# A convolution with residual on one core: first load on one ring, 4 MB residual loads and stores, fewer semaphores

## The chip, the cores and the metric

The kernel runs on one core of one Trainium2 chip. The time is the device time in microseconds. A profile is one execution, and its span, from the first to the last instruction of the program, is some 1.9 us shorter than the time (121.2 us against 123.0 for the profiled execution before). All instants below are microseconds from the span's start. PE runs the matmuls, ACT and DVE cast and add, GpSimd (POOL) makes constants and clears semaphores, and SP issues transfers. A "ring" is the queue of transfers of one issuing engine; in the profiles q1 is that of SP and q10 that of ACT.

## The reference

A 3x3 convolution with padding 1, batch 16, 64 channels in and out, 64x64 pixels, all float32, plus a residual of the output's shape:

```python
x_pad = np.pad(x, ((0, 0), (0, 0), (pad, pad), (pad, pad)), mode='constant')
...
output[b, co] += weight[co, ci, kh, kw] * x_pad[b, ci, kh:kh+h, kw:kw+w]
...
return (output + residual).astype(np.float32)
```

x, the residual and the output have 16.8 MB each; the weights have 0.15 MB. So 50.48 MB cross between HBM and the core, in either kernel.

## The kernel before

The images go in pairs: two images of 64 channels fill the 128 partitions, so one pair of x, of the residual or of the output is 2 MB (128 rows of 16 KB). ACT casts x to bf16 in two halves per image, PE makes six accumulating groups of four matmuls per image in one of two halves of PSUM, and DVE adds PSUM to the residual in place with two instructions per image. SP issues nearly all transfers, in the program's order:

```python
def load_x(p, engine=nc.sync, cols=slice(0, NPIX)):
    return engine.dma_start(out=xr[p % NXR][:, cols], in_=x_bc[128 * p : 128 * p + 128, cols]).then_inc(
        s_x[p % NXR], 16
    )

def load_ro(p):
    nc.sync.dma_start(out=ro[p][:, :], in_=res_bc[128 * p : 128 * p + 128, :]).then_inc(s_r[p], 16)

def store(p):
    return nc.sync.dma_start(out=out_bc[128 * p : 128 * p + 128, :], in_=ro[p][:, :])
# ... cut ...
for p in range(NPAIR):                       # NPAIR = 8, NXR = 3 buffers of x
    if p >= NXR:
        nc.sync.wait_ge(s_half, 2 * (p - NXR) + 3)   # ACT is done with the buffer
    if p == 0:
        to_the_front(load_x(p, cols=slice(0, NPIX // 2)))
        nc.sync.dma_start(out=wraw[:, :], in_=w_rows[:, :]).then_inc(s_w, 16)
    else:
        load_x(p)
    load_ro(p)
for p in range(NEARLY):                      # NEARLY = 6
    nc.sync.wait_ge(s_add, 2 * p + 3)
    store(p).then_inc(s_out, 16)
# ... cut: GpSimd's constants ...
to_the_front(load_x(0, nc.scalar, slice(NPIX // 2, NPIX)))   # the second half, on ACT's ring
# ... cut: ACT's casts, DVE's adds, PE's loop ...
for p in range(NEARLY, NPAIR):               # after the critical section
    store(p)
with tc.tile_critical(sync_engine=mybir.EngineType.Pool, no_gpsimd_drain=True):
    nc.gpsimd.wait_ge(s_out, 16 * NEARLY)
```

`to_the_front` moves a load ahead of the program's first barrier, so that it starts at once. After the program's last transfer come two barriers of all engines with a clear of the kernel's semaphores between them, which the language adds.

## Time and profile before

| | before |
|---|---|
| time, median of 3 runs | 123.09 us (122.86 to 123.21) |
| span | 121.2 us |
| PE, DVE, ACT busy | 72%, 63%, 52% |
| bytes between HBM and core, mean over the span | 50.48 MB, 417 GB/s |
| DMAs of the program | 26 (x 9, weights 1, residual 8, output 8) |
| last add ends, last two stores issued | 104.1; 104.4 and 104.8 |
| last two stores landed | 115.4 and 120.2 |

The timeline of the kernel before, from the last adds on, without the sequencers' waits (start, duration, engine and line, operation, count):

```profile
99.52 4.61 DVE L201 TENSOR_TENSOR ro<-ps,ro 64x2048 f32<-64x2048 f32 x2 [0.58 <-PE ps L86]
104.42 0.96 SPq L79 DMA_DIRECT2D out_dram<-ro  x2
```

The reader is to see that no engine works after 104.1, and that issuing the last two stores takes SP less than a microsecond. The remaining 16 us hold no instruction that computes; they are all transfers. The prediction below shows the page's slices and reads them.

### The profile page before, as it was taken

What the parts mean: (1) busy time and instruction counts of PE and PEld (TensorE: products, weight loads), DVE (VectorE), ACT (ScalarE), POOL (GpSimd) and SP (SyncE); (2) the same over time, 40 slices, a digit from 0 to 9 for tenths busy, and PEclk for the clock granted to TensorE, in tenths of its full rate; (3) what the DMA queues carried; (4) which work ended last, traced back from release to release, by engine and by line L of the source; (5) the groups of instructions that cost most, each with busy time, mean ns of one, the idle gap of its engine ahead of it and who ended that gap; (6) DMA issues with size and microseconds to landing.
All of it is one profiled execution on the core that took longest, in us unless ns stands there. A gap on an engine that the chain in (4) does not pass through costs nothing.

```text
span 121.2 us, 736 instructions
## 1 busy us (share of the span) xinstructions
PE 87.7 (72%) x389; PEld 10.7 (9%) x105; DVE 76.0 (63%) x40; ACT 63.1 (52%) x37; POOL 2.4 (2%) x16
## 2 busy tenths in 40 slices
PE   0033499999999999999999999999999980000000
PEld 0021001101010101010101010101010100000000
DVE  0005300889898898989889898898989889300000
ACT  4049969938966984993993994896000000000000
POOL 5200000000000000000000000000000000000000
PEclk9999999999999999999999999999999999755555
DMA  6999999999999999999999999999999999999993
GB/s 168 427 444 433 433 433 433 433 427 433 433 427 427 433 433 427 427 433 427 433 433 433 433 433 422 433 389 433 433 433 433 422 433 433 433 433 433 427 433 151
DMA packets 3744, 50.48 MB, mean 417 GB/s; under 512 B 416, under 2 KB 544, under 8 KB 544
## 3 DMA queue, kind: packets, MB, share of 16 engines
q1 hardware_dynamic: 3600, 49.43, 96.3%
q10 hardware_dynamic: 144, 1.05, 2.0%
HBM read 33.70 MB, written 16.78 MB: 417 GB/s over the span
## 4 chain that ended last, share of the span: by engine, by line
PE 71%; DVEq 2%; DVE 2%; issue 0%
PE ps L86 53%; PE ps L85 17%; DVEq L129 2%; DVE ro L201 2%
## 5 line engine op out<-in xcount | busy, mean ns | idle before, releaser
L201 DVE TENSOR_TENSOR ro<-ps,ro 64x2048 f32<-64x2048 f32 x32 | 73.2, 2289 | 17.7 <-PE ps L86 17.2
L86 PE MATMUL ps<-xp,wl 128*128 128x504 bf16 (+1 forms) x288 | 80.0, 388 | 0.2
L173 ACT CAST xp<-xr 64x2048 bf16<-64x2048 f32 x16 | 30.3, 1896 | 19.3 <-DMA xr<-in_x_dram 17.1
L85 PE MATMUL ps<-xp,wl 128*128 128x504 bf16 (+1 forms) x92 | 35.8, 389 | 3.4 <-PEq L222 3.4
L177 ACT CAST xp<-xr 64x2048 bf16<-64x2048 f32 x16 | 30.4, 1897 | 0.4
L85 PEld LDWEIGHTS ps<-xp,wl 128*128 128x128 bf16 x96 | 9.5, 99 | 79.1 <-issue 79.1
L189 DVE CAST wl<-ps 32x192 bf16<-32x192 f32 x8 | 2.8, 348 | 10.4 <-PE ps L214 10.3
L214 PE MATMUL ps<-ident,wraw 128*32 128x128 f32 x9 | 2.1, 412 | 8.1 <-DMA wraw<-in_weight_dram 8.1
L214 PEld LDWEIGHTS ps<-ident,wraw 128*32 128x32 f32 x9 | 1.2, 137 | 8.6 <-issue 8.1
L173 ACT ACT_TABLE_LOAD x1 | 1.3, 1283 | 1.1 <-SPq L129 1.1
L182 ACT CAST wl<-ps 32x192 bf16<-32x192 f32 x4 | 1.2, 306 | 0.0
L160 POOL MEMSET xp<- 64x64 bf16 x4 | 0.6, 147 | 0.2
L159 POOL MEMSET xp<- 64x64 bf16 x4 | 0.6, 145 | 0.2
L148 POOL TENSOR_SCALAR_AFFINE_SELECT ident<-ident 128x128 f32<-128x128 f32 x1 | 0.3, 295 | 0.2 <-POOL ident L146 0.2
L162 POOL MEMSET wl<- 64x192 bf16 x1 | 0.3, 253 | 0.1
L161 POOL MEMSET wl<- 64x192 bf16 x1 | 0.3, 252 | 0.1
L146 POOL MEMSET ident<- 128x128 f32 x1 | 0.2, 205 | 0.7 <-SPq L129 0.7
L257 POOL MEMSET const-uint8-127<- 128x1 uint8 x1 | 0.1, 113 | 0.0
L257 POOL MEMSET const-bfloat16-1.0<- 128x1 bf16 x1 | 0.1, 112 | 0.0
L257 POOL MEMSET const-float32-1.0<- 128x1 f32 x1 | 0.1, 109 | 0.0
L257 POOL MEMSET const-float32-0.0<- 128x1 f32 x1 | 0.1, 104 | 0.2 <-issue 0.2
## 6 DMA issues: line engine op xcount, KB each, us to landing
ro<-in_residual_dram SPq DMA_DIRECT2D x8, 2048.0 KB, 21.9
out_dram<-ro SPq DMA_DIRECT2D x8, 2048.0 KB, 28.2
xr<-in_x_dram SPq DMA_DIRECT2D x7, 2048.0 KB, 17.5
xr<-in_x_dram SPq DMA_DIRECT2D x1, 1024.0 KB, 7.0
xr<-in_x_dram ACTq DMA_DIRECT2D x1, 1024.0 KB, 7.6
wraw<-in_weight_dram SPq DMA_DIRECT2D x1, 144.0 KB, 6.9
```

Of the source, the lines that this page charges most:

```text
L85: return e.matmul(out=out_, lhsT=lhsT, rhs=rhs, start=start, stop=stop, skip_group_check=True)
L86: return e.add_instruction(mybir.InstMatmult(name=nc.get_next_instruction_name(), engine=PE, ins=[e.lower_ap(rhs), e.lower_ap(lhsT)], outs ...
L129: with tc.tile_critical(no_gpsimd_drain=True):
L159: nc.gpsimd.memset(t[0:64, 0, :], 0.0).then_inc(s_id, 1)
L160: nc.gpsimd.memset(t[64:128, J, :], 0.0).then_inc(s_id, 1)
L173: i = nc.scalar.copy(out=t[64:128, 0:J, :], in_=x4[hp, :, 0, :])
L177: nc.scalar.copy(out=t[0:64, 1 : J + 1, :], in_=x4[hp, :, 1, :]).then_inc(s_pack, 1)
L182: i = nc.scalar.copy(**weight_block(h, *b))
L189: i = nc.vector.tensor_copy(**weight_block(h, *b))
L201: i = nc.vector.tensor_tensor(out=o4[hp, :, par, :], in0=psj[64 * par : 64 * par + 64, :, :], in1=o4[hp, :, par, :], op=ADD)
L214: i = nc.tensor.transpose(out=tp[0:32, t // 3, 128 * (t % 3) : 128 * (t % 3) + 128], in_=wraw3[:, :, t], identity=ident[:, :])
L257: nc = _bacc.Bacc("TRN2", target_bir_lowering=False, num_devices=1)
```

## The change

The intent was to hand the same bytes to the transfers in fewer pieces: a first load of x on one ring, residual loads and early stores of two pairs (4 MB), fewer semaphores, and a clear of the user's semaphores on GpSimd while the last stores still run. The core of the diff:

```diff
-    NEARLY = 6
+    NEARLY = 3
+    RES = (slice(0, 1), slice(1, 2), slice(2, 4), slice(4, 6), slice(6, 8))
-    res_bc = residual.rearrange("b c h w -> (b c) (h w)")
+    res_bc = residual.rearrange("(p b) c h w -> (b c) p (h w)", b=2)
-    ro = [pool.tile([128, NPIX], FP32, name=f"ro{p}") for p in range(NPAIR)]
+    ro = pool.tile([128, NPAIR, NPIX], FP32)
-    s_r = [sem(f"s_r{p}") for p in range(NPAIR)]
+    s_r = [sem(f"s_r{i}") for i in range(2)]
-    s_wt = sem("s_wt")
...
+    def load_ro(i):
+        if i >= 2:
+            nc.sync.wait_ge(s_r[i % 2], 16 * (i // 2))
+        nc.sync.dma_start(out=ro[:, RES[i], :], in_=res_bc[:, RES[i], :]).then_inc(s_r[i % 2], 16)
+    def store(pairs):
+        return nc.sync.dma_start(out=out_bc[:, pairs, :], in_=ro[:, pairs, :])
...
-                to_the_front(load_x(p, cols=slice(0, NPIX // 2)))
+                to_the_front(load_x(p))
...
-            load_ro(p)
-        for p in range(NEARLY):
-            nc.sync.wait_ge(s_add, 2 * p + 3)
-            store(p).then_inc(s_out, 16)
+            if p in (0, 1, 3, 5, 7):
+                load_ro((p + 1) // 2)
+        for k in range(NEARLY):
+            nc.sync.wait_ge(s_add, 4 * k + 5)
+            store(slice(2 * k, 2 * k + 2)).then_inc(s_out, 16)
...
-        to_the_front(load_x(0, nc.scalar, slice(NPIX // 2, NPIX)))
...
         nc.gpsimd.wait_ge(s_out, 16 * NEARLY)
+        tc.free_semaphores([s_w, *s_x, *s_r, s_out, s_id, s_half, s_pack, s_bank, s_conv, s_add])
```

The cuts hold the same change for the output's view, the use of `s_id` in place of `s_wt`, and the indices that follow from them.

More of the change, by code (lines that the diff above doesn't have):

```diff
@@ L37 @@
     NXP = 4
-    NEARLY = 6
-    res_bc = residual.rearrange("b c h w -> (b c) (h w)")
-    out_bc = out.rearrange("b c h w -> (b c) (h w)")
+    NZERO = 4 + 2 * NXP
+    NEARLY = 3
+    RES = (slice(0, 1), slice(1, 2), slice(2, 4), slice(4, 6), slice(6, 8))
+    res_bc = residual.rearrange("(p b) c h w -> (b c) p (h w)", b=2)
+    out_bc = out.rearrange("(p b) c h w -> (b c) p (h w)", b=2)
     x_bc = x.rearrange("b c h w -> (b c) (h w)")
@@ L68, with load_x @@
     s_add = sem("s_add")
-    def load_x(p, engine=nc.sync, cols=slice(0, NPIX)):
-        return engine.dma_start(out=xr[p % NXR][:, cols], in_=x_bc[128 * p : 128 * p + 128, cols]).then_inc(
-            s_x[p % NXR], 16
-        )
-    def load_ro(p):
-        nc.sync.dma_start(out=ro[p][:, :], in_=res_bc[128 * p : 128 * p + 128, :]).then_inc(s_r[p], 16)
-    def store(p):
-        return nc.sync.dma_start(out=out_bc[128 * p : 128 * p + 128, :], in_=ro[p][:, :])
+    def load_x(p):
+        return nc.sync.dma_start(out=xr[p % NXR][:, :], in_=x_bc[128 * p : 128 * p + 128, :]).then_inc(s_x[p % NXR], 16)
+    def load_ro(i):
[4 more added lines that the diff above has]
+        return nc.sync.dma_start(out=out_bc[:, pairs, :], in_=ro[:, pairs, :])
     def matmul(out_, lhsT, rhs, start, stop, ldweights):
@@ L171 @@
             if im == 0:
-                nc.scalar.wait_ge(s_x[p % NXR], 16 * (p // NXR + 1 + (p % NXR == 0)))
+                nc.scalar.wait_ge(s_x[p % NXR], 16 * (p // NXR + 1))
             i = nc.scalar.copy(out=t[64:128, 0:J, :], in_=x4[hp, :, 0, :])
@@ L178 @@
             if n == 0:
-                nc.scalar.wait_ge(s_wt, 1)
+                nc.scalar.wait_ge(s_id, NZERO + 1)
                 for b in blocks[4:]:
@@ L182 @@
                         i = nc.scalar.copy(**weight_block(h, *b))
-                i.then_inc(s_wt, 1)
-        nc.vector.wait_ge(s_wt, 1)
+                i.then_inc(s_id, 1)
+        nc.vector.wait_ge(s_id, NZERO + 1)
         for k, b in enumerate(blocks[:4]):
@@ L191 @@
                     i.then_inc(s_bank, 2)
-        i.then_inc(s_wt, 1)
+        i.then_inc(s_id, 1)
         for n in range(B):
@@ L195 @@
             hp = slice(64 * im, 64 * im + 64)
-            o4 = ro[p].rearrange("q (j two w) -> q j two w", two=2, w=W)
+            o4 = ro[:, p, :].rearrange("q (j two w) -> q j two w", two=2, w=W)
             psj = ps[n % 2].rearrange("q c j w -> q (c j) w")
             if im == 0:
-                nc.vector.wait_ge(s_r[p], 16)
+                i = next(i for i, pairs in enumerate(RES) if p < pairs.stop)
+                nc.vector.wait_ge(s_r[i % 2], 16 * (i // 2 + 1))
             for par in range(2):
@@ L207 @@
                 i.then_inc(s_add if par == 0 or n == B - 1 else s_bank, 1)
-        nc.tensor.wait_ge(s_id, 4 + 2 * NXP)
+        nc.tensor.wait_ge(s_id, NZERO)
         nc.tensor.wait_ge(s_w, 16)
@@ L216 @@
             )
-        i.then_inc(s_wt, 1)
-        nc.tensor.wait_ge(s_wt, 3)
+        i.then_inc(s_id, 1)
+        nc.tensor.wait_ge(s_id, NZERO + 3)
         with nc.Fori(0, B // NXP, 1, engines=[PE]):
@@ L236 @@
                 m.then_inc(s_conv, 1)
-    for p in range(NEARLY, NPAIR):
-        store(p)
+    for p in range(2 * NEARLY, NPAIR):
+        store(slice(p, p + 1))
     with tc.tile_critical(sync_engine=mybir.EngineType.Pool, no_gpsimd_drain=True):
         nc.gpsimd.wait_ge(s_out, 16 * NEARLY)
+        tc.free_semaphores([s_w, *s_x, *s_r, s_out, s_id, s_half, s_pack, s_bank, s_conv, s_add])
 _INS = ['x', 'weight', 'residual']
```

## The prediction

> **What bounds the kernel now.** I read the page's slices first, because the ladder of engines (PE 72%, DVE 63%, ACT 52%) names no engine that is full. The slices and the queue table do:
>
> ```profile
> PE   0033499999999999999999999999999980000000
> DVE  0005300889898898989889898898989889300000
> DMA  6999999999999999999999999999999999999993
> GB/s 168 427 444 433 433 433 433 433 427 433 433 427 427 433 433 427 427 433 427 433 433 433 433 433 422 433 389 433 433 433 433 422 433 433 433 433 433 427 433 151
> ...
> q1 hardware_dynamic: 3600, 49.43, 96.3%
> q10 hardware_dynamic: 144, 1.05, 2.0%
> ```
>
> The reader is to see that DMA stands at 9 in every slice but the first and the last, at about 433 GB/s, while PE is idle in the last seven slices and DVE in the last five. The chain of work on the page says "PE 71%", but it follows instructions only; it stops at the last stores' issue and doesn't see that these stores then queue behind others. The DMA queue's own waits and the stretches show that:
>
> ```profile
> SPq L268 <- DMA out_dram<-ro: 14.8, 2, 10.0
> ```
>
> ```profile
> 1.00:2.00 1.00, 0.00 (x0) 0.00 (x0) 0.00 (x0) 0.92 (x1) 0.59 (x3) 1.00 1.06 197
> 2.00:3.00 1.00, 0.00 (x0) 0.00 (x0) 0.00 (x0) 0.36 (x1) 0.73 (x6) 1.00 0.84 311
> 3.00:4.00 1.00, 0.00 (x0) 0.00 (x0) 0.00 (x0) 0.00 (x0) 0.78 (x5) 1.00 1.00 418
> ...
> 110.00:115.00 5.00, 0.00 (x0) 0.00 (x0) 0.00 (x0) 0.00 (x0) 0.00 (x0) 0.50 0.99 423
> ```
>
> The last add ends at 104.1 us and the last two stores are issued at 104.42 and 104.80, yet they land at 115.4 and 120.2, because earlier stores (2 MB each, 4.85 us from one landing to the next) still stand in front: the sixth lands at 110.5. So compute has about 5 us of slack at the end: a 2 MB store whose data reaches the queue before the sixth store leaves it, near 110, costs nothing.
>
> The account of the 121.2 us is then: first packet at 1.0 us after the span's start; 50.48 MB at the steady 433 GB/s, which is 116.6 us; a ramp (197, 311 and 418 GB/s in the three microseconds from 1.0 on) that loses (236 + 122 + 15)/433 = 0.86 us; a dip at 78 us (389 GB/s in one slice of 3.03 us, 0.3 us lost), where the loads end and the stores begin; and a tail of about 1.3 us: the last data packet ends at 119.87, the last landing is at 120.2, and two barriers of all engines with a semaphore clear of 0.20 us between them run to 121.17. The sum is 1.0 + 116.6 + 0.9 + 0.3 + 1.3 = 120.1, one short of the span, the rest being smaller dips and engines that end some 0.3 us apart. The time measured (123.09) is 1.9 us more than the span and stays out of the kernel's reach.
>
> **What the Trainium skill says, and whether this trace agrees.** "DMA: Bandwidth & Descriptors", section Specifications, gives 435 GB/s as the fabric's ceiling for one core's 16 engines; the trace's 433 GB/s agrees, so there is no bandwidth left to win. The same page, section "Issuing engines are not separate DMA queues", says that transfers of several issuing engines share the same 16 DMA engines and interleave, so a second one only saves issue time. The trace agrees: 434 GB/s with both rings in use (4 to 6 us) and 433 later with one. The same page, "Anatomy of one DMA", calls the semaphore write's bubble tiny; here each 4-byte semaphore packet has 9 ns, and neighbouring 16 KB packets (611 ns each) follow it without a gap. "Perfetto Trace Analysis", section on the HWDGE instruction, says that the completion write waits until the data write is confirmed; the 0.34 us from the last data packet's end to its landing is of that kind, and the change keeps one such tail.
>
> **The change part by part.**
>
> *One-ring first load.* Before, x of pair 0 comes as two 1 MB halves, on the SP ring and the ACT ring. After, SP issues all 2 MB. The same bytes move. With two rings, the weights (144 KB) and part of the first residual on the SP ring alternate with the second half on the ACT ring, so x lands at 7.75 and the weights at 8.01. With one ring x comes first: it and the weights are 2.24 MB or 5.2 us behind an average start of about 1.5 us, with landing some 0.4 us on: about 7.1 us. Everything of PE may start 0.6 us sooner, at about 13 instead of 13.66; PE goes on at 5.19 us an image (DVE's adds begin at 94.33 and 99.52). That gain falls in the slack and is worth nothing. For the DMA engines, 16 packets of 309 ns become 8 of 611 each: 4.94 against 4.89, 0.05 us. The ramp's 0.86 us might shrink or grow by a few tenths as ACT no longer asks for descriptors beside SP: I take -0.1, and this is a choice.
>
> *4 MB residual loads.* Eight loads become five (1, 1, 2, 2, 2 pairs). Same bytes, and still 16 KB runs, since a pair's rows lie 2 MB from the next pair's in HBM. With the stores (eight to five) that is seven DMAs fewer after one more is saved in x: 26 to 19, seven semaphore packets of 5 to 9 ns fewer on each engine: 0.04 to 0.06 us. The order alters: x3 passes ahead of ro2, and ro2 and ro3 land together. Counting 2 MB per 4.85 us from the observed landings (12.9 for ro0, 17.8 for x1, 22.6 for ro1): x2 27.5, x3 32.3, ro2-3 42.0, x4 46.9, x5 51.7, ro4-5 61.5, x6 66.4, x7 71.2, ro6-7 81.0. DVE's adds need ro2 for image 4, ro4 for image 8 and ro6 for image 12, which begin at 42.46, 63.21 and 83.96 before, by PE's pace. Moved 0.6 us forward that is 41.9, 62.6 and 83.4: the first may wait 0.1 to 0.3 us, the others have 1.1 and 2.4 us to spare. No loss.
>
> *SP's new waits.* SP waits for ro0 before ro2-3, for ro1 before ro4-5 and for ro2-3 (42.0) before ro6-7. The question is whether the queue runs dry meanwhile. x3 needs image 2's first cast, 17.8 + 1.9 = 19.7, when the queue holds work to 27.2; x4 needs image 4's, 27.5 + 1.9 = 29.4, against 41.8; x5 about 37 (ACT is in order: four casts of 1.9 us behind x2, then one) against 46.7; x6 about 48.9 against 61; x7 about 56.5 against 66. ro6-7 follows x7. None runs dry; the least margin is 7 us.
>
> *Early stores of two pairs.* They wait for image 4's, 8's and 12's first add, 44.5, 65.5 and 86.3 before. The loads occupy the queue to 81.0, then the stores 9.7 us each: to 90.7, 100.4 and 110.1. The third is ready at 86, needed at 100. The last two pairs go singly as before, issued at about 104. No starvation, so the end of the data stays.
>
> *Clear while stores run, and fewer semaphores.* In the built program the GpSimd clears 13 semaphores before the end, but the last clear between the barriers is still there; its range is 99 to 120 (22) instead of 99 to 127 (29). At 0.20 us for 29 it saves some 0.05 us if it goes by count. Both barriers stay. The added clear comes after the seventh store's landing and some 4 us before the eighth's, so it is hidden.
>
> *DVE's waits.* In both kernels DVE waits on a residual once per pair; the order of its instructions is the same (21 rows each). Worth nothing.
>
> Sum: -0.1 (ramp) -0.05 (packets) -0.05 (semaphore packets) -0.05 (clear) = -0.25 us: 122.84, say 122.8.
>
> **The rivals.** (a) *Starvation*: a residual that comes late in the 4 MB order stops DVE, hence PE's PSUM buffers, ACT, x loads. The landings above speak against it: 5 us of slack at the end and 7 us in the queue. If the order cost over 5 us of compute, each us beyond would add one. Most likely it costs nothing. (b) *4 MB transfers slower than 2 MB*: consecutive packets of an engine now alternate between two places 2 MB apart in HBM. Nothing in the trace tests this; if the 611 ns packets became 620, 184 of them per engine would add 1.7 us, giving 124.5. Against it: reads and writes run at the same 611 now, which suggests that HBM isn't what limits. (c) *The ramp and the dip move*: both together lose about 1.2 us, so the two can give at most this: a best case of 121.6. (d) *The tail is what matters*: had the early clear replaced the final one and a barrier, it would save about 0.5 us; the built program keeps both, so this is not expected.
>
> **Range and chances.** All parts that lie on the transfers' path are tenths of a microsecond; the three runs before spread over 0.35 us. Range 122.2 to 123.3. The 2% bounds are 120.6 and 125.6: the lower one needs twice what (c) holds, the upper needs (b) worse than guessed. Faster 0.01, same 0.97, slower 0.02.
>
> **What would show it right or wrong.** Right: slices of DMA at 9 throughout, 433 GB/s, 50.48 MB, packets at 611 ns; x and weights landing near 7; last stores landing within 0.4 us of 115.4 and 120.2 with compute done by 104.5; the last clear near 0.15 us; a span of about 120.9. Wrong: a slice of DMA under 9 between 25 and 105 us (starvation, then DVE's wait names the residual load), packets over 611 ns beside 4 MB transfers, a ramp that reaches 430 GB/s earlier by more than half a microsecond, or a tail after the last landing that isn't near 0.95 us.

## The result and the profile after

| | before | after |
|---|---|---|
| median | 123.12 us (122.86 to 123.30, 6 runs) | 122.72 us (122.68 to 122.88, 6 runs) |
| ratio, 95% interval | | 0.9971 (0.9958 to 0.9984) |
| span of the profiled execution | 121.17 us | 120.85 us |
| x of pair 0 and the weights landed | 7.75 and 8.01 | 7.77 and 8.13 |
| first matmul of the convolution | 13.66 | 13.78 |
| last load landed | 81.26 | 81.14 |
| last two stores landed | 115.36 and 120.21 | 115.10 and 119.95 |
| last landing to the end of the span | 0.96 us | 0.90 us |
| semaphores in the last clear, its duration | 29, 0.20 us | 22, 0.15 us |

A ratio here is the mean time of one kernel's fast runs over that of the other's of the same rounds, so it is not quite the ratio of the medians. The change was a gain of 0.29%, within the 2% that counts as the same. In a later set of rounds the changed kernel came to 0.9982 (0.9969 to 0.9995). So the gain is 0.22 to 0.36 us (0.18% and 0.29% of 123.1), and its interval excludes zero in both sets.

The page of the changed kernel, engines' and transfers' slices, and its only DMA queue:

```profile
PE   0024499999999999999999999999999990000000
DVE  0005400789898988989879898988989879500000
DMA  7999999999999999999999999999999999999994
GB/s 168 428 428 428 428 428 434 428 434 434 428 434 434 434 428 434 434 434 434 434 434 423 423 428 434 423 412 434 434 434 434 423 434 434 434 428 434 434 434 174
...
q1 hardware_dynamic: 3504, 50.48, 98.5%
```

The picture is that of before: DMA at 9 throughout, the compute engines done early, 50.48 MB at 423 to 434 GB/s but for the two ends and one slice. One queue carries it all now. The slice of 412 GB/s stands where 389 stood before.

The DMA queue's own waits of the changed kernel (who waited, for whom; total us, times, longest):

```profile
SPq L72 <- ACT xp L174: 50.9, 5, 16.3
SPq L80 <- DVE ro L203: 27.9, 2, 20.3
SPq L130 <- DVEq L130: 17.4, 1, 17.4
SPq L271 <- DMA out_dram<-ro: 14.3, 2, 9.5
```

No line names a residual load: none of SP's waits was ended by the new conditions on `s_r`. As before, SP waits at the end for stores that are still under way, now for 14.3 us where it was 14.8.

The first stretches and one near the end, changed kernel (window, engines' busy time, PE clock, DMA share, GB/s):

```profile
1.00:2.00 1.00, 0.00 (x0) 0.00 (x0) 0.00 (x0) 1.00 (x1) 0.66 (x4) 1.00 1.62 295
2.00:3.00 1.00, 0.00 (x0) 0.00 (x0) 0.00 (x0) 0.24 (x1) 0.73 (x6) 1.00 0.58 213
3.00:4.00 1.00, 0.00 (x0) 0.00 (x0) 0.00 (x0) 0.00 (x0) 0.78 (x4) 1.00 0.90 377
...
110.00:115.00 5.00, 0.00 (x0) 0.00 (x0) 0.00 (x0) 0.00 (x0) 0.00 (x0) 0.50 0.99 423
```

A packet's bytes and time are counted where it starts, so with 16 KB packets the rows of one microsecond swing more than they did with 8 KB ones. Added up, they are 885 KB over the three microseconds against 926 before (GB/s times us are KB), so in this profile the ramp (the slow first microseconds of the transfers) lost 41/433, about 0.1 us, more and not less; x of pair 1 landed 0.11 us later too. In b0, a later profile of the same program, the three rows come to 982 KB, so this is not yet a property of the kernel.

And the end of the changed kernel's timeline:

```profile
99.67 4.61 DVE L203 TENSOR_TENSOR ro<-ps,ro 64x2048 f32<-64x2048 f32 x2 [0.58 <-PE ps L87]
104.58 0.98 SPq L80 DMA_DIRECT2D out_dram<-ro  x2
```

Compute ended 0.15 us later than before, at 104.28, and yet the kernel ended 0.32 us sooner. That speaks against compute setting the end; b3 and b4 below test it.

### The profile page after: what moved, and what is told of

The parts are those of the page before. It is cut to its first block, busy times and chain, and to the rows that moved or that the text cites. A ratio compares the mean times of both kernels' runs of the same rounds, so it can differ in the third digit from the quotient of the medians.

```text
span 120.8 us, 734 instructions
## 1 busy us (share of the span) xinstructions
PE 87.9 (73%) x393; PEld 10.7 (9%) x105; DVE 76.0 (63%) x40; ACT 63.1 (52%) x37; POOL 2.4 (2%) x16
## 2 busy tenths in 40 slices
DMA packets 3504, 50.48 MB, mean 418 GB/s; under 512 B 304, under 2 KB 432, under 8 KB 432
## 3 DMA queue, kind: packets, MB, share of 16 engines
q1 hardware_dynamic: 3504, 50.48, 98.5%
## 4 chain that ended last, share of the span: by engine, by line
PE 71%; DVEq 2%; DVE 2%; issue 0%
PE ps L87 53%; PE ps L86 18%; DVEq L130 2%; DVE ro L203 2%
## 5 line engine op out<-in xcount | busy, mean ns | idle before, releaser
L87 PE MATMUL ps<-xp,wl 128*128 128x504 bf16 (+1 forms) x288 | 80.0, 388 | 0.0
L86 PE MATMUL ps<-xp,wl 128*128 128x504 bf16 (+1 forms) x96 | 37.4, 389 | 3.4 <-PEq L224 3.4
```

The costliest lines, as they stand in the source:

```text
L86: return e.matmul(out=out_, lhsT=lhsT, rhs=rhs, start=start, stop=stop, skip_group_check=True)
L87: return e.add_instruction(mybir.InstMatmult(name=nc.get_next_instruction_name(), engine=PE, ins=[e.lower_ap(rhs), e.lower_ap(lhsT)], outs ...
```

## The experiments

Each is timed against the kernel before in the same rounds. The diffs are excerpts, without the indices and waits that follow from them. Where two experiments of one set are compared, their ratios are subtracted and the difference is taken of 123.0 us. The sets ran on different chips, so landings of two sets are compared with care. The question was which parts make the 0.22 to 0.36 us, whether compute really has slack, and where the dip near 78 us comes from. "Turn" below is the passage from loads to stores in the queue, and the "turn's loss" is what the last 4 MB of loads took from landing to landing, less 4.85 us per 2 MB.

**First set: one part alone, added to the kernel before (before: median 123.16 us).**

*a1_onering*: the first load on one ring.

```diff
-                to_the_front(load_x(p, cols=slice(0, NPIX // 2)))
+                to_the_front(load_x(p))
-        to_the_front(load_x(0, nc.scalar, slice(NPIX // 2, NPIX)))
```

> The kernel before with one part of the change alone: the first x is loaded whole on SP's ring. The prediction's theory counted -0.15 us for it (ramp -0.1, packets -0.05). The two traces say otherwise: x0 and the weights landed 0.02 and 0.12 us later in the changed kernel, and the loads up to 71 us too. So theory 'ramp gains' expects 122.95 to 123.0 and weights near 7.5; theory 'ramp costs a tenth' expects 123.1 to 123.2, weights at 8.1 and every later landing 0.1 later.

Measured: 123.31 us (122.88 to 123.56), ratio 1.0008 (0.9987 to 1.0028). In its profile x landed at 8.12, the weights at 8.45, and ro0 at 13.32 against 12.88. The single ring brings no gain of 0.15 us that could be seen; whether it costs a tenth the interval leaves open. Its runs spread wider than any other kernel's.

*a2_res4*: the residual in five loads, each with its own semaphore.

```diff
-            load_ro(p)
+            if p in (0, 1, 3, 5, 7):
+                load_ro((p + 1) // 2)
```

> The kernel before with the residual in five loads (1, 1, 2, 2, 2 pairs), each with a semaphore of its own, nothing else changed. The prediction's theory counts only 3 semaphore packets per engine: -0.02 us, so no change to be seen. A rival, from the traces: the dip near 78 us, at the end of the loads, shrank from 0.36 to 0.11 us of lost time per engine, and it is the 4 MB loads that did this; then -0.2 to -0.25 us and a landing of the last residual near 81.0.

Measured: 123.00 us (122.89 to 123.29), ratio 0.9990 (0.9974 to 1.0006). The last load landed at 81.23. The profile shows the turn's loss as 0.13 us, but the interval holds "nothing" as well as the rival's -0.2 us.

*a3_store4*: six early stores as three.

```diff
-            store(p).then_inc(s_out, 16)
+            store(slice(2 * k, 2 * k + 2)).then_inc(s_out, 16)
```

> The kernel before with the six early stores as three of 4 MB, nothing else changed. The prediction's theory: -0.02 us, nothing to be seen. A rival: the dip at the end of the loads depends on the first stores queued behind them; then -0.2 us, with the last residual landing near 81.0 and not 81.26.

Measured: 123.17 us (123.08 to 123.30), ratio 1.0003 (0.9989 to 1.0017); the last load landed at 81.45. Nothing gained; the rival is out, as a gain of 0.2 us (0.9984) lies outside the interval.

*a4_sems*: only the semaphores and the early clear.

```diff
-    s_r = [sem(f"s_r{p}") for p in range(NPAIR)]
+    s_r = [sem(f"s_r{i}") for i in range(2)]
-    s_wt = sem("s_wt")
+        if p >= 2:
+            nc.sync.wait_ge(s_r[p % 2], 16 * (p // 2))
+        tc.free_semaphores([s_w, *s_x, *s_r, s_out, s_id, s_half, s_pack, s_bank, s_conv, s_add])
```

> The kernel before with the semaphore part alone: two residual semaphores in turn (SP waits for the load two before), the weights' semaphore merged into another, 13 user semaphores instead of 20, the early clear. All transfers as before. The prediction's theory: last clear 0.15 instead of 0.20 us, so -0.05 us and a stretch of 0.89 us from the last landing to the end; no starvation from SP's waits. Rival: the waits hold back a load, and DMA falls under 9 tenths in some slice, +0.1 us or more.

Measured: 122.97 us (122.81 to 123.15), ratio 0.9987 (0.9973 to 1.0001). From the last landing (120.09) to the end of the span (120.98) it took 0.89 us, and the clear 0.15 us, as expected; DMA stays at 9 in every slice but the first and last. That is so although SP was held by the new waits, six times and for 21.9 us in all:

```profile
SPq L78 <- DMA ro<-in_residual_dram: 21.9, 6, 9.3
```

The transfers already in the queue covered the delay, so the rival is out. The sign is that of a gain; that it is more than the 0.05 us of the clear is not shown.

**Second set: one part taken back from the changed kernel (before: median 123.07 us).**

*b0_after*: the changed kernel again, with a comment added.

> The changed kernel again, as the measure for the three that follow in the same rounds. All theories: ratio to before near 0.997, 122.7 to 122.8.

Measured: 122.83 us (122.77 to 123.10), ratio 0.9982 (0.9969 to 0.9995). In this profile the turn's loss was 0.46 us (71.30 to 81.46); in the first profile of the same program it was none (71.47 to 81.14). The start moved too: x landed at 7.62 here and at 7.77 there. So these terms change between executions of one program, and no single look can tell what a change does to them.

*b1_tworing*: the first x in two halves on two rings again (the inverse of the diff of a1).

> The changed kernel with the first x again in two halves on two rings. Adding the single ring to the kernel before alone gave +0.08% with a wide spread (122.88 to 123.56). Theory 'one ring costs a tenth at the start': 122.6 to 122.7, 0.1 under the changed kernel, x0 landing at most 0.1 earlier. The prediction's theory (one ring gains 0.15): 122.9. Theory 'start varies by itself, no part in it': equal within 0.1.

Measured: 123.00 us (122.91 to 123.08), ratio 0.9995 (0.9982 to 1.0008); x landed at 7.71 against 7.62 in b0. Here one ring is ahead by 0.0013, or 0.16 us; in the first set it was behind by 0.0008, or 0.10 us. The two differ in sign and their intervals hold zero or overlap: "no part in it that these rounds can see" is what stays.

*b2_nofree*: without the early clear.

```diff
-        tc.free_semaphores([s_w, *s_x, *s_r, s_out, s_id, s_half, s_pack, s_bank, s_conv, s_add])
```

> The changed kernel without the early clear; the 13 user semaphores stay as few, so the last clear keeps its range of 22. The prediction's theory: the early clear is hidden under the last store and the final clear covers its semaphores anyway, so no change (within 0.05 us), last clear still 0.15 us. Rival: semaphores cleared early make the last clear cheaper; then this run is slower by 0.05 us or more and its clear longer.

Measured: 122.80 us (122.71 to 122.96), ratio 0.9982 (0.9969 to 0.9995), the same ratio as b0; last clear 0.16 us. The early clear is worth nothing that can be seen: it removes nothing from the last one, which covers the same 22 semaphores with it or without it.

*b5_two_mb*: 2 MB residual loads and stores again.

```diff
-    RES = (slice(0, 1), slice(1, 2), slice(2, 4), slice(4, 6), slice(6, 8))
+    RES = tuple(slice(p, p + 1) for p in range(NPAIR))
-            store(slice(2 * k, 2 * k + 2)).then_inc(s_out, 16)
+            store(slice(k, k + 1)).then_inc(s_out, 16)
```

> The changed kernel with 2 MB residual loads and 2 MB stores again (SP's waits on the two residual semaphores stay). The prediction's theory: six DMAs more, +0.03 us, nothing to be seen. Rival: the 4 MB transfers are where the measured gain over the predicted parts came from; then +0.1 to +0.2 us.

Measured: 122.93 us (122.83 to 123.11), ratio 0.9989 (0.9977 to 1.0001), 0.09 us more than b0. That lies between the two expectations and inside the noise. With a2 and a3 it says that the size of the transfers, 2 or 4 MB, is worth about a tenth by the means; the intervals hold nothing as well as two tenths.

**Third set: the slack, the turn, the clear (before: median 123.00 us).**

*b3_slack1* and *b4_slack4*: one and four extra adds of the same form between DVE's last two, into a buffer that is no longer used.

```diff
                 i.then_inc(s_add if par == 0 or n == B - 1 else s_bank, 1)
+                if n == B - 1 and par == 0:
+                    for k in range(4):       # range(1) in b3_slack1
+                        part = xr[0][64 * (k // 2) : 64 * (k // 2) + 64, NPIX // 2 * (k % 2) : NPIX // 2 * (k % 2) + NPIX // 2]
+                        part = part.rearrange("q (j w) -> q j w", w=W)
+                        nc.vector.tensor_tensor(out=part, in0=psj[0:64, :, :], in1=part, op=ADD)
```

> The changed kernel with one more add of the same form on DVE (2.29 us, PSUM and a spare buffer in, the spare buffer out) between the last two adds, so that DVE ends at about 106.6 instead of 104.3. Result unaltered. The prediction's theory (5 us of slack at the end): no change, 122.7 to 122.9, the last stores issued near 106.9 and 107.3 and landing as before near 115.1 and 120.0. Rival 'the last stores' issue is on the path': +2.3 us, 125.1.

> The same with four extra adds (9.16 us), so that the last stores are issued near 113.8. The sixth pair's store leaves the queue at about 109.9, so the slack is used up: a store issued into an empty queue takes 1.0 us to its first packet, 4.85 us of packets and 0.35 us to land, so it lands near 120.0 and the last near 124.9: +4.9 us, 127.6; a slice of DMA falls well under 9. Rival (compute is the path all along): +9.2 us.

Measured: with one add 122.94 us (122.82 to 123.03), ratio 0.9988 (0.9967 to 1.0009), so 2.29 us more of compute cost nothing that can be seen (the changed kernel itself was not run in this set; its ratios in the other two, 0.9971 and 0.9982, lie inside this interval). With four it was 127.55 us (127.50 to 127.90), ratio 1.0364 (1.0343 to 1.0385), 4.62 us over b3. The slices of b4 show why:

```profile
DVE  0006100989889898898988989889889899990000
DMA  7999999999999999999999999999999999705994
GB/s 183 422 443 428 422 422 438 443 433 428 422 428 433 448 428 428 422 428 438 443 428 433 422 422 438 438 428 417 433 417 443 443 433 422 334 0 250 454 459 172
```

DVE is busy through slice 36, and in that slice DMA stands at 0 for the first time (0 GB/s). The queue stood empty from 110.06 to 114.45 us, that is 4.39 us. The slack of the changed kernel's compute is therefore 9.16 - 4.62 = 4.5 us, near the 5 that the prediction read off the landings.

*c1_mix*: one store ahead of the last residual load.

```diff
+            if p == 7:
+                nc.sync.wait_ge(s_add, 3)
+                store(slice(0, 1)).then_inc(s_out, 16)
```

(and the other early stores as 1, 2 and 2 pairs.)

> The changed kernel with the store of pair 0 (2 MB) put ahead of the last residual load, so that the queue goes loads, a store, a load, stores: three turns between directions instead of one. Asked: where the dip near 78 us comes from. It has lost the slowest engine between 0 and 0.45 us in different executions. If it belongs to the turn from loads to stores, slow packets come near 69 (some 2 us before x7's end at 71.2) and perhaps again near 83, and the time is the same or up to 0.3 us longer. If it belongs to a fixed time of the program, they stay at 77 to 80. DVE waits about 2 us for the last residual (86.0 instead of 81.1), inside its slack, so no other loss.

Measured: 123.13 us (123.03 to 123.36), ratio 1.0013 (0.9996 to 1.0030). Two stretches of 1.5 us tell where the slow packets are. Kernel before:

```profile
69.00:70.50 1.50, 1.50 (x9) 0.10 (x1) 1.50 (x1) 1.48 (x2) 0.00 (x0) 1.00 1.07 459
...
78.00:79.50 1.50, 1.50 (x9) 0.19 (x2) 0.92 (x2) 1.48 (x2) 0.00 (x0) 1.00 0.99 328
```

c1_mix:

```profile
69.00:70.50 1.50, 1.50 (x9) 0.19 (x2) 1.48 (x1) 1.50 (x1) 0.00 (x0) 1.00 0.97 382
...
78.00:79.50 1.50, 1.50 (x9) 0.19 (x2) 0.93 (x1) 1.14 (x2) 0.00 (x0) 1.00 1.02 437
```

The last number of each row is GB/s. Before, the low one is at 78; with a store ahead of the last load it is at 69. The packets agree: eleven of over 640 ns start from 69.0 to 70.1, one more at 70.4, none from 77 to 80, and one at 84.5 ahead of the second passage to stores. So the dip goes with the passage from loads to stores (its slow packets start 1.1 to 3.6 us ahead of the load's landing in these two profiles) and not with a time of the program. It doesn't come at every passage: the second one has a single slow packet. What makes it is not shown. The expected DVE wait was too small: DVE waited 3.1 us for the last residual, not 2; its last add began at 105.8 and still came in time for the queue.

*c2_sems*: 90 more semaphores, allocated and not used.

```diff
+    for k in range(90):
+        sem(f"s_spare{k}")
```

> The changed kernel with 90 more semaphores allocated and never used, so that the last clear covers 112 semaphores instead of 22. Theory: the clear goes by count, 0.11 us for 13, 0.15 for 22, 0.18 for 26 and 0.20 for 29 so far, that is 0.0056 us for one, and it lies on the path: last clear 0.65 us, time +0.5 us (123.3). Rival: the clear takes no longer or is hidden: no change.

Measured: 123.46 us (123.34 to 123.64), ratio 1.0033 (1.0011 to 1.0055), 0.55 us over b3. The last clear took 0.63 us for 112 semaphores, so 0.48/90 = 0.0053 us for each. The drain ahead of it grew too, from 0.09 to 0.21 us. From the last landing to the end it took 1.50 us instead of 0.90. The clear's length is on the path, and it goes by the number of semaphores allocated.

No version beat the changed kernel: b2_nofree equals it (both 0.9982), and each other was behind it by less than the intervals, or slower.

## Why the prediction was right or wrong

The time was predicted as 122.8 us, a gain of 0.25 us or 0.20%. Measured were 122.72 us and gains of 0.29% and, in the later set, 0.18%. By its steps:

- **The bound: right, its account not quite.** Compute slack was given as about 5 us; b3 and b4 measure 4.5. The transfers ran at the same rate in both kernels, with 611 ns for a 16 KB packet. The account of the span came out one microsecond short, and "smaller dips" were blamed. The landings say that two of its terms were too small. From ro0's to ro6's (12.88 to 71.29 us) 25.17 MB moved at 431 GB/s, not 433, so all bytes take 117.1 us. At that rate, and with 0.35 us from the last packet to the landing, the 4.34 MB up to ro0 would have had to start at 2.46 us to land at 12.88; so the ramp costs an estimated 1.5 us after the first packet at 1.0, and not the 0.86 read from rows that credit a packet's bytes to its start. With 0.28 us at the turn and 1.3 us at the end, 2.46 + 117.1 + 0.28 + 1.3 gives 121.1.
- **No starvation: right.** The predicted landings came true within 0.3 us (ro2-3 42.0 and 42.19, x5 51.7 and 51.98, ro6-7 81.0 and 81.14, stores 90.7, 100.4, 110.1 and 90.87, 100.53, 110.24), and so did the issues (x5 "about 37" and 37.31, x7 "about 56.5" and 56.78). DVE's waits in the changed kernel name PE and no residual load. Rival (a) is out. (Image 4's first add ended at 44.74 us before, not 44.5; nothing hangs on it.)
- **4 MB transfers as fast as 2 MB: right.** Packets stay at 611 ns, and a2, a3 and b5 differ from their partners by 0.12 us at most. Rival (b) is out.
- **One-ring load: wrong, in two terms.** The step that failed is "about 7.1 us" for the landing of the first x and "Everything of PE may start 0.6 us sooner", and with it "-0.1" for the ramp. x landed at 7.77, and the convolution began at 13.78 instead of 13; so its own sign "x and weights landing near 7" did not come. I had counted 2.24 MB at full rate after an average start of 1.5 us. In the changed kernel's profile sixteen packets were under way at once by 1.28 us (1.99 before), but the first sixteen took 719 to 2034 ns instead of 611. The other eight profiles with one ring had sixteen under way only by 1.4 to 2.4 us and those with two rings by 1.6 to 2.1, and in the kernel before the first packets were slow too (8 KB in up to 1295 ns instead of 309). So the loss sits in the first packets, with one ring or two, and no run shows that the ring changes it. What makes them slow is not shown. PE's missing head start cost nothing, as the prediction said that this part lies in the slack; a1 and b1 put the whole term at +0.10 and -0.16 us, so it is not told from zero.
- **The clear: right.** 22 semaphores took 0.15 us, the tail went from 0.96 to 0.90 us, and c2 confirms both the price for one and that it is on the path. Of the rivals, (d) was rightly set aside: b2 without the early clear has the same time. The clear while the last stores run does nothing that can be seen; the seven semaphores saved do.
- **The dip: right in place, wrong as a constant.** The prediction took 0.3 us at the passage from loads to stores as fixed. It moves between 0 and 0.46 us from one execution to the next of one program (after and b0). Between the two profiled spans, 0.32 us apart, the turn gave 0.31: the last 4 MB of loads took 9.98 us before and 9.67 after. The stretch ahead of it took 0.18 away (0.11 of it by 17.9 us), the stores from there on gave 0.14, and the tail 0.06. So those two profiles don't explain the measured gain, though their difference is nearly the same number.

What makes up the 0.22 to 0.36 us is thus settled in part. About 0.05 us is the shorter clear. The rest, 0.17 to 0.31, is not assigned: seven DMAs fewer, one ring, or the turn on average. Each of these alone is below what five rounds resolve (the intervals are some 0.15 to 0.25 us to each side), and I leave it open. The kept profiles give a hint and no more. The turn's loss is 0.17 to 0.34 us in the five with 2 MB residual loads (mean 0.26), and -0.03 to 0.46 in the eight with 4 MB (mean 0.15; c1 left out). x of pair 1 landed at 17.71 to 17.86 in the five with two rings and at 17.74 to 18.24 in the nine with one. So larger loads may save a tenth at the turn and one ring may cost a tenth at the start, but the ranges overlap.

That the sum of -0.25 us fell between the two measured gains is therefore in part luck. Of its four terms (-0.1, -0.05, -0.05, -0.05) only the clear's is shown, the ramp's did not come, the two for packets are too small to see, and something not assigned made up the rest.

## What to carry to other kernels

When the transfers run at one rate from end to end, count bytes and landings first, and ask of each part of a change whether it alters the bytes, the start, the end, or only work that has slack; what is left is then tenths of a microsecond. "Same" is safe on that ground, the sum of the tenths is not. Test slack directly, by adding work until the queue runs dry: 2.3 us more cost nothing that could be seen, 9.2 us cost 4.6. Do not explain a difference of 0.3 us from one profile each, when a second profile of the same program moves the same term by 0.5 us.

## What the Trainium skill lacked or had wrong

- "DMA: Bandwidth & Descriptors": has nothing on the passage from loads to stores on the same engines. Here packets of up to 1202 ns (b0) instead of 611 start from some 3.6 us (before) ahead of the last load's landing, at a cost of 0 to 0.46 us, changing between executions.
- "DMA: Bandwidth & Descriptors", Latency and other measured facts, gives about 600 ns to the first byte on this path. Here the first packet started 1.01 us after SP began to issue, that is 0.62 after the end of the issuing instruction (0.38 us), and a store into an empty queue (b4) 0.85 us after its issue began, 0.50 after the end of that instruction (0.35 us). So the figure fits roughly if it is counted from the end of the issue, and is short if it is counted from its beginning. What the page lacks is what follows: the program's first sixteen packets took 719 to 2034 ns in the changed kernel where later ones take 611, while those of the store in b4 took 608 to 626, so not every start is slow.
- "Runtime: NRT & Kernel Launch", The ~15µs preamble/postamble breakdown, prices a reset of semaphores that the runtime adds after the kernel. Neither it nor another page gives the price of the clear that the language puts at the program's end: 0.11 us for 13, 0.15 for 22, 0.20 for 29, 0.63 for 112, with a drain ahead of it that grew from 0.09 to 0.21 us.
